# Recurrent unit of a two-layer encoder: twelve turns instead of thirteen, two products on other engines, extra turns under the other gate group

## The chip, the cores and the metric

The kernel runs on one core of a Trainium2 chip. A core has five engines with a queue each: TensorE (PE in the profile; its weight loads are listed apart as PEld), VectorE (DVE), ScalarE (ACT), GpSimd (POOL) and SyncE (SP), which here issues most DMAs. Each engine takes its own instructions in order and waits for the others by semaphores. The metric is the device time of one execution in microseconds.

## What is computed

Two layers over one sequence of 512 positions with 2048 features, in float32. The first layer (the one that the change touches) projects the normalised input into attention heads, a recurrent branch and gates, and mixes them:

```python
xc = lax.conv_general_dilated(x_lru, conv_w[:, None, :], ..., feature_group_count=LRU_WIDTH) + conv_b
y = (rg_lru(xc, wa[0], ba[0], wx[0], bx[0], lam[0], reverse=False)
     + rg_lru(xc, wa[1], ba[1], wx[1], bx[1], lam[1], reverse=True))
mix = jnp.concatenate([attn * jax.nn.silu(g_attn), y * jax.nn.silu(g_lru)], axis=-1)
return mix @ w_out
```

with, in `rg_lru` (one direction, 1024 channels in 8 blocks of 128):

```python
r = jax.nn.sigmoid(einsum(xb, wa) + ba)
i = jax.nn.sigmoid(einsum(xb, wx) + bx)
log_a = LRU_C * r * jax.nn.log_sigmoid(lam)
a = jnp.exp(log_a)
u = jnp.sqrt(-jnp.expm1(2.0 * log_a)) * (i * xc)
_, h = lax.associative_scan(lru_combine, (a, u), reverse=reverse, axis=1)   # h = a * h_before + u
```

The second layer is an mLSTM with its own projections; nothing in it is changed.

## The kernel before

**Bulk products.** All large products run in groups of 512 output columns, in steps that the code calls chunks (`NCH` = 8 per group, 256 input rows each). A weight chunk of 128 x 1024 values is loaded by SP's queue into one of three buffers (`raw`), and split into a high half `wh` (ACT, L153) and a low half `wl` (VectorE, L154), because each product is made of three passes on PE. Loads are issued three chunks ahead and splits two chunks ahead of PE (`self.ahead(i, 3, 2)`), with four buffers for the halves. A chunk of a first-layer group is 24 matmuls of 512 columns on PE, into four PSUM banks; at the last chunk the four banks are evacuated.

**Order of the groups in layer 1.** keys and values; Q0; L0 and L1 (input of the recurrence); Q1; GL0 and GL1 (gates of the recurrence, L809 and L810: a product on VectorE, a silu on ACT); GA0 and GA1 (gates of attention, same evacuation); then four groups of the output projection.

**Two lanes of small work.** While a group runs, other work is fed between its chunks from two lanes of Python generators; each `yield` ends a turn. Lane 0 (`pump(0)`) has one turn per chunk: key and query preparation, then attention (`attn_gen`: score product S, maximum L787 and L788 on VectorE, exp L791 on ACT, reciprocal L792 on VectorE, scaling L793 on ACT, transposes, split into `pth` and `ptl`, product PV). Lane 1 (`pump(1)`) has one turn at the end of each chunk: the four recurrent units `lru_gen(0)` to `lru_gen(3)`, one after the other. A group with the field `more=n` gives lane 1 a further turn, after bank 0, in each of its first n chunks. GA0 has `more=8` and GA1 none.

**A recurrent unit** handles two blocks (j) in two directions (d), each 128 x 512. Its 13 turns: two of convolution (`conv`), four of gates (`gates`: six matmuls "lg" on PE, then L880 on VectorE), one with four sigmoids (L895) and tanh (L900) on ACT and the input product i * xc on GpSimd (L903); one with exp on ACT (L908), its square on GpSimd (L911) and (square + 1) * tanh on VectorE (L912); an empty one; one with the square root on ACT (L917) and its product with the input on GpSimd (L918, 128 x 1024 each); an empty one; then the scans, a forward and a backward one per j on VectorE (L923, L925), and their sum y on GpSimd (L927), with j = 0 and j = 1 in a turn each. At the end `value_ready` multiplies y with its gate on VectorE (L832) where the gate is there already; else it stores y to DRAM (L824), to be loaded again (L818, 512 KB each way) when the gate is evacuated.

Counted by chunks, the turns of lane 1 are: 1 at L0's last chunk, 2 to 9 in L1, 10 to 17 in Q1, 18 to 25 in GL0, 26 to 33 in GL1, 34 to 49 in GA0 (two per chunk), 50 to 57 in GA1. Units 0 to 3 take turns 1 to 13, 14 to 26, 27 to 39 and 40 to 52. So unit 0's y goes through DRAM, unit 1's does not (its last turn is in GL1's first chunk).

**Splits of the mixed values.** Each chunk of the output projection needs its input split into `oh` (ACT) and `ol` (VectorE), by `mix_split`. From GA1's first chunk on, one such split stands ahead of each weight split, in the order attention 0, 1, recurrence 0, 1, 2, 3.

**Program order and issue order.** The framework orders each engine's instructions by priority (earlier in the program first) among those that its own model takes for ready. So an instruction can be issued ahead of one that stands before it in the program, and turns that lie apart can run in one block. Evacuations have a raised priority.

The activation function table of ACT is reloaded (ACT_TABLE_LOAD) where the next function isn't in the one loaded.

Of the kernel before, what the change touches and what calls it, by code (L numbers as in the profile page):

```python
# [15 lines left out]
AF = mybir.ActivationFunctionType  # L16
ALU = mybir.AluOpType
# [484 lines left out]
class Layer1(Builder):  # L502
# [344 lines left out]
    def lru_gen(self, i):  # L847
        nc, pb, v = self.nc, self.pb, self.nc.vector
        xp = self.xpad[i]
        xc = self.slot2("xc")  # L850
        hl, wh, wl = [None] * 2, [None] * 2, [None] * 2
        rr, ii = [None] * 2, [None] * 2

        def conv(j):
            b = 2 * i + j
            w = self.half("lwr")
            nc.sync.dma_start(out=w, in_=self.a["lru_w"][b])
            nc.scalar.activation(xc[:, j, :], xp[:, j, 0:512], AF.Identity,
                                 bias=pb[:, PB_CB + b:PB_CB + b + 1],
                                 scale=pb[:, PB_CW + 4 * b:PB_CW + 4 * b + 1])  # L860
            for t in range(1, 4):
                v.scalar_tensor_tensor(out=xc[:, j, :], in0=xp[:, j, t:t + 512],
                                       scalar=pb[:, PB_CW + 4 * b + t:PB_CW + 4 * b + t + 1],
                                       in1=xc[:, j, :], op0=ALU.mult, op1=ALU.add)
            hl[j] = self.slot2("xchl", F32R)
            self.split(hl[j][:, 0, :], hl[j][:, 1, :], xc[:, j, :])
            ws = self.slot2("lws", F32R)
            self.split(ws[:, 0, :], ws[:, 1, :], w)
            wh[j], wl[j] = ws[:, 0, :], ws[:, 1, :]

        def gates(j, d):
            b = 2 * i + j
            if d == 0:
                rr[j], ii[j] = self.slot2("lr"), self.slot2("li")
            for gi, (dst, off) in enumerate(((rr, PB_BA), (ii, PB_BX))):
                ps = self.psum("lg")
                ws = slice((2 * gi + d) * P, (2 * gi + d + 1) * P)
                self.mm3(ps, wh[j][:, ws], wl[j][:, ws], hl[j][:, 0, :], hl[j][:, 1, :])
                col = off + 2 * b + d
                v.tensor_scalar(out=dst[j][:, d, :], in0=ps, scalar1=pb[:, col:col + 1], scalar2=None, op0=ALU.add)  # L880

        conv(0)
        yield
        conv(1)
        yield
        gates(0, 0)
        yield
        gates(0, 1)
        yield
        gates(1, 0)  # L890
        yield
        gates(1, 1)
        yield
        for t in (rr[0], rr[1], ii[0], ii[1]):
            nc.scalar.activation(t, t, AF.Sigmoid)  # L895
        tau = [self.slot2("ltau") for j in range(2)]
        for j in range(2):
            for d in range(2):
                c = 2 * (2 * i + j) + d
                nc.scalar.activation(tau[j][:, d, :], rr[j][:, d, :], AF.Tanh, scale=self.lamc[:, c:c + 1])  # L900
        for j in range(2):
            for d in range(2):
                nc.gpsimd.tensor_tensor(out=ii[j][:, d, :], in0=ii[j][:, d, :], in1=xc[:, j, :], op=ALU.mult)  # L903
        yield
        for j in range(2):
            for d in range(2):
                c = 2 * (2 * i + j) + d
                nc.scalar.activation(rr[j][:, d, :], rr[j][:, d, :], AF.Exp, scale=self.lamn[:, c:c + 1])  # L908
            for d in range(2):
                e2 = self.half("le2")  # L910
                nc.gpsimd.tensor_tensor(out=e2, in0=rr[j][:, d, :], in1=rr[j][:, d, :], op=ALU.mult)  # L911
                v.scalar_tensor_tensor(out=tau[j][:, d, :], in0=e2, scalar=1.0, in1=tau[j][:, d, :],  # L912
                                       op0=ALU.add, op1=ALU.mult)
        yield
        yield
        for j in range(2):
            nc.scalar.activation(tau[j], tau[j], AF.Sqrt)  # L917
            nc.gpsimd.tensor_tensor(out=ii[j], in0=ii[j], in1=tau[j], op=ALU.mult)  # L918
        yield
        yield  # L920
        y = self.slot2("y")
        for j in range(2):
            v.tensor_tensor_scan(out=tau[j][:, 0, :], data0=rr[j][:, 0, :], data1=ii[j][:, 0, :],  # L923
                                 initial=0.0, op0=ALU.mult, op1=ALU.add)
            v.tensor_tensor_scan(out=tau[j][:, 1, ::-1], data0=rr[j][:, 1, ::-1], data1=ii[j][:, 1, ::-1],  # L925
                                 initial=0.0, op0=ALU.mult, op1=ALU.add)
            nc.gpsimd.tensor_tensor(out=y[:, j, :], in0=tau[j][:, 0, :], in1=tau[j][:, 1, :], op=ALU.add)  # L927
            if j == 0:
                yield
        self.mixv[4 + i] = y  # L930
        self.value_ready(4 + i)
        yield
# [57 lines left out]
class Layer2(Layer1):  # L990
# [549 lines left out]
    def build(self):  # L1540
# [14 lines left out]
        w1, wo1, w2, wo2 = a["even_w_in"], a["even_w_out"], a["odd_w_in"], a["odd_w_out"]  # L1555

        def grp(w, lo, lay, x, evac, **kw):
            return dict(w=w[:, lo:lo + 512], lay=lay, x=x, evac=evac, **kw)
# [18 lines left out]
        x1 = self.x1s.__getitem__  # L1577
# [6 lines left out]
        def after_q(g):  # L1584
            def f():
                add(0, self.q_gen(g))
                add(0, self.attn_gen(g))
            return f
# [6 lines left out]

        L = [grp(w1, 2560 + 512 * g, "T", x1, self.xlru_evac(g), after=after_lru(g)) for g in range(2)]
        Q = [grp(w1, 512 * g, "tok", x1, self.q_evac(g), after=after_q(g)) for g in range(2)]
        GA = [grp(w1, 1536 + 512 * g, "T", x1, self.gate_evac(2 * g), more=8 - 8 * g) for g in range(2)]
        GL = [grp(w1, 3584 + 512 * g, "T", x1, self.gate_evac(4 + 2 * g)) for g in range(2)]
        groups += [Q[0], L[0], L[1], Q[1], GL[0], GL[1], GA[0], GA[1]]  # L1600

# [183 lines left out]
```

## Time and profile before

| what | value | where from |
|---|---|---|
| median of 3 runs | 1645.04 us (1641.71 to 1645.58) | times |
| profiled execution | 1641.33 us, its span 1639.6 us | times, page |
| scans of unit 0 start at | 218.6, 219.8, 220.9, 222.0 us | timeline of VectorE |
| scans of unit 1 start at | 292.7, 293.9, 309.5, 310.7 us | timeline of VectorE |
| scans of unit 2 start at | 403.6, 407.5, 408.7, 409.8 us | timeline of VectorE |
| scans of unit 3 start at | 469.0, 472.3, 481.9, 483.0 us | timeline of VectorE |
| gates evacuated: GL0, GL1, GA0 (first to last) | 319.9 to 324.5, 380.8 to 385.2, 453.6 to 458.1 us | timeline of VectorE |
| PV of an attention pair on PE | 1.4 us, 12 matmuls | chain that ended last |
| four transposes on PE | 0.4 us | chain that ended last |

The profiled execution is one of four that are known; three others were only timed. All durations in the prediction come from the profiled one. Columns of a timeline: start in us, length in us, engine, line, operation, output <- inputs, shape, and in brackets the idle time of the engine before it and what ended that. A span of a GpSimd or VectorE instruction includes time in which it could not read its operands.

### The profile page before, as it was taken

The page shows a single profiled execution, that of the slowest core. Times are in us where ns is not written, and L with a number is a line of the kernel's source. Part 1 is how long each engine was busy: PE and PEld are TensorE (multiplying, and loading weights), DVE is VectorE, ACT ScalarE, POOL GpSimd, SP SyncE. Part 2 cuts the span into 40 slices and gives each one's busy share as a digit, 9 for nine tenths or more (in the row PEclk, how much of TensorE's full clock was granted, in tenths as well). Part 3 has the DMA queues.
Part 4 walks back from the last instruction along what each step waited for, and adds up shares of the span by engine and source line. Part 5 has one row for each costly group of instructions (what it writes and reads, how often), then busy time and mean ns, then how long its engine had stood idle before and what let it go on. Part 6 is the DMA issues. An engine that isn't in the chain of part 4 may idle for free.

```text
span 1639.6 us, 25389 instructions
## 1 busy us (share of the span) xinstructions
PE 1610.4 (98%) x9698; PEld 1424.1 (87%) x9698; DVE 1122.1 (68%) x1714; ACT 850.1 (52%) x1395; POOL 745.6 (45%) x732
## 2 busy tenths in 40 slices
PE   9999999999989999999999999999999999999997
PEld 7888888888768888889999999999988888888997
DVE  8755476855774333457999986666777577668976
ACT  6334665667763333334445443444576466665453
POOL 5220122303130111386698778888611322368872
PEclk9999999999989999999999999999999999999999
DMA  6433133321324544644444443444554444452565
GB/s 229 134 93 98 52 103 103 92 88 52 107 71 157 178 169 155 200 140 126 121 129 138 133 142 106 129 134 134 184 168 126 129 153 142 153 182 80 142 176 176
DMA packets 138698, 218.12 MB, mean 133 GB/s; under 512 B 9792, under 2 KB 62400, under 8 KB 138576
## 3 DMA queue, kind: packets, MB, share of 16 engines
q1 hardware_dynamic: 136304, 213.80, 41.5%
q0 software_dynamic: 1088, 2.10, 0.8%
q8 instruction: 76, 1.25, 0.3%
q10 hardware_dynamic: 1184, 0.60, 0.1%
q14 instruction: 46, 0.38, 0.1%
HBM read 182.36 MB, written 34.11 MB: 132 GB/s over the span
## 4 chain that ended last, share of the span: by engine, by line
PE 83%; DVE 6%; ACT 4%; POOL 3%; issue 3%; DMA 1%; SPq 0%; DVEq 0%; POOLq 0%; ACTq 0%
PE bk L157 44%; PE s L157 29%; DVE wl L154 2%; PE nb L157 2%; PE nf L157 1%; PE PV L157 1%; PE ST L157 1%; PE lg L157 1%; PE S L157 1%; PE tr L160 1%; ACT wh L153 1%; PE gt L157 0%; DMA hTr<-hTd 0%; DVE ltau L923 0%; DVE ltau L925 0%
## 5 line engine op out<-in xcount | busy, mean ns | idle before, releaser
L154 DVE TENSOR_TENSOR wl<-raw,wh 128x1024 fp32r<-128x1024 f32 (+3 forms) x333 | 363.4, 1093 | 267.4 <-ACT wh L153 266.7
L153 ACT CAST wh<-raw 128x1024 fp32r<-128x1024 f32 (+3 forms) x333 | 265.9, 800 | 435.7 <-PE s L157 224.5
L363 POOL TENSOR_TENSOR w7s<-raw 128x256 f32<-128x256 f32 x216 | 222.5, 1048 | 95.5 <-DMA raw<-in_odd_w_in_dram 68.2
L154 DVE TENSOR_TENSOR wl<-w7s,wh 128x512 fp32r<-128x512 f32 (+1 forms) x176 | 203.7, 1158 | 6.3 <-ACT wh L153 6.3
L157 PE MATMUL bk<-xh,wl 128*128 128x512 f32 x384 | 152.1, 396 | 5.7 <-DVE wl L154 5.7
L157 PE MATMUL s<-th,wl 128*128 128x256 f32 x544 | 153.2, 282 | 0.8 <-DVE wl L154 0.8
L157 PE MATMUL s<-th,wh 128*128 128x256 f32 x544 | 152.7, 281 | 0.5 <-ACT wh L153 0.5
L157 PE MATMUL s<-tl,wh 128*128 128x256 f32 x544 | 153.0, 281 | 0.0
L157 PE MATMUL bk<-xh,wh 128*128 128x512 f32 x384 | 152.2, 396 | 0.0
L157 PE MATMUL bk<-xl,wh 128*128 128x512 f32 x384 | 152.0, 396 | 0.0
L153 ACT CAST wh<-w7s 128x512 fp32r<-128x512 f32 (+1 forms) x176 | 125.6, 714 | 17.9 <-POOL w7s L363 17.9
L363 POOL TENSOR_TENSOR w7s<-w7s,raw 128x256 f32<-128x256 f32 x108 | 120.3, 1114 | 0.0
L157 PE MATMUL s<-bh,wh 128*128 128x256 f32 x408 | 115.3, 283 | 0.9 <-ACT wh L153 0.9
L157 PE MATMUL s<-bh,wl 128*128 128x256 f32 x408 | 114.8, 281 | 0.3 <-DVE wl L154 0.3
L157 PE MATMUL s<-bl,wh 128*128 128x256 f32 x408 | 114.4, 280 | 0.0
L903 POOL TENSOR_TENSOR li<-li,xc 128x512 f32<-128x512 f32 x16 | 21.4, 1361 | 191.9 <-ACT li L895 191.9
L363 POOL TENSOR_TENSOR w7s<-raw,w7s 128x256 f32<-128x256 f32 x108 | 101.1, 936 | 7.8
L157 PEld LDWEIGHTS s<-th,wl 128*128 128x128 f32 x544 | 102.8, 189 | 1.3 <-DVE wl L154 1.3
L157 PEld LDWEIGHTS s<-th,wh 128*128 128x128 f32 x544 | 102.4, 188 | 0.7 <-ACT wh L153 0.7
L157 PEld LDWEIGHTS s<-tl,wh 128*128 128x128 f32 x544 | 102.5, 188 | 0.0
L157 PE MATMUL bk<-oh,wh 128*128 128x512 f32 x256 | 101.0, 394 | 0.0
L157 PE MATMUL bk<-ol,wh 128*128 128x512 f32 x256 | 100.8, 394 | 0.0
(349 smaller groups left out, 4532.6 us busy)
## 6 DMA issues: line engine op xcount, KB each, us to landing
raw<-in_odd_w_in_dram SPq DMA_DIRECT2D x120, 512.0 KB, 3.9
raw<-in_even_w_in_dram SPq DMA_DIRECT2D x71, 512.0 KB, 3.7
raw<-in_even_w_out_dram SPq DMA_DIRECT2D x32, 512.0 KB, 3.7
raw<-in_odd_w_out_dram SPq DMA_DIRECT2D x32, 512.0 KB, 3.7
xres<-in_xT_dram SPq DMA_DIRECT2D x8, 512.0 KB, 6.4
x2d<-xres SPq DMA_DIRECT2D x8, 512.0 KB, 4.3
xgd<-xg SPq DMA_DIRECT2D x8, 512.0 KB, 4.0
xr<-xgd SPq DMA_DIRECT2D x8, 512.0 KB, 7.3
```

Source lines behind the costliest of these rows:

```text
L153: self.nc.scalar.copy(h, x)
L154: (eng or self.nc.vector).tensor_tensor(out=l, in0=x, in1=h.bitcast(F32), op=ALU.subtract)
L157: self.nc.tensor.matmul(out, a, b, start=start, stop=stop)
L160: self.nc.tensor.transpose(out, x, ident)
L363: po.tensor_tensor(out=s[:, :, q, :], in0=x, in1=y, op=op)
L903: nc.gpsimd.tensor_tensor(out=ii[j][:, d, :], in0=ii[j][:, d, :], in1=xc[:, j, :], op=ALU.mult)
```

## The change

It has five parts, all in layer 1.

1. The product of the root with the input (L918) is issued on VectorE instead of GpSimd.
2. The square of the exponential (L911) is issued on ACT instead of GpSimd.
3. The sum y of j = 1 is issued on VectorE instead of GpSimd; that of j = 0 stays.
4. The empty turn before the root goes, and the two turns behind it become one between root and product and one between product and scans: 12 turns per unit instead of 13.
5. GA0 no longer has additional lane-1 turns (`more=0`), and GA1 has them in its first four chunks (`more=4`).

Counted again, lane 1 has turns 34 to 41 in GA0 (one per chunk), 42 to 49 in GA1's chunks 0 to 3 (two per chunk) and 50 to 53 in its chunks 4 to 7. Units 0 to 3 take turns 1 to 12, 13 to 24, 25 to 36 and 37 to 48.

```diff
@@ -908,15 +908,15 @@
             for d in range(2):
                 e2 = self.half("le2")
-                nc.gpsimd.tensor_tensor(out=e2, in0=rr[j][:, d, :], in1=rr[j][:, d, :], op=ALU.mult)
+                nc.scalar.activation(e2, rr[j][:, d, :], AF.Square)
                 v.scalar_tensor_tensor(out=tau[j][:, d, :], in0=e2, scalar=1.0, in1=tau[j][:, d, :],
                                        op0=ALU.add, op1=ALU.mult)
         yield
-        yield
         for j in range(2):
             nc.scalar.activation(tau[j], tau[j], AF.Sqrt)
-            nc.gpsimd.tensor_tensor(out=ii[j], in0=ii[j], in1=tau[j], op=ALU.mult)
-        yield
+        yield
+        for j in range(2):
+            v.tensor_mul(ii[j], ii[j], tau[j])
         yield
         y = self.slot2("y")
         for j in range(2):
...
-            nc.gpsimd.tensor_tensor(out=y[:, j, :], in0=tau[j][:, 0, :], in1=tau[j][:, 1, :], op=ALU.add)
+            (v if j else nc.gpsimd).tensor_tensor(out=y[:, j, :], in0=tau[j][:, 0, :], in1=tau[j][:, 1, :], op=ALU.add)
             if j == 0:
                 yield
...
-        GA = [grp(w1, 1536 + 512 * g, "T", x1, self.gate_evac(2 * g), more=8 - 8 * g) for g in range(2)]
+        GA = [grp(w1, 1536 + 512 * g, "T", x1, self.gate_evac(2 * g), more=4 * g) for g in range(2)]
```

More of the change, by code (lines that the diff above doesn't have):

```diff
@@ L914, in lru_gen @@
         yield
+        for j in range(2):
+            nc.scalar.activation(tau[j], tau[j], AF.Sqrt)
         yield
         for j in range(2):
-            nc.scalar.activation(tau[j], tau[j], AF.Sqrt)
-            nc.gpsimd.tensor_tensor(out=ii[j], in0=ii[j], in1=tau[j], op=ALU.mult)
-        yield
+            v.tensor_mul(ii[j], ii[j], tau[j])
         yield
```

## The prediction

> **What bounds the kernel now.** I read the page first, then windows along the span, then what TensorE (PE) waited for, then short windows around its two holes, and last the rows of the engines that made those holes.
>
> ```profile
> span 1639.6 us, 25389 instructions
> ...
> PE 1610.4 (98%) x9698; PEld 1424.1 (87%) x9698; DVE 1122.1 (68%) x1714; ACT 850.1 (52%) x1395; POOL 745.6 (45%) x732
> ...
> 200.00:400.00 200.00, 199.60 (x960) 164.65 (x959) 133.69 (x196) 130.56 (x187) 48.75 (x36) 1.00 0.28 85
> ...
> 400.00:450.00 50.00, 46.33 (x215) 37.71 (x214) 35.84 (x51) 35.50 (x53) 12.05 (x8) 0.97 0.34 102
> 450.00:500.00 50.00, 43.30 (x192) 35.32 (x191) 34.24 (x32) 29.57 (x35) 14.26 (x9) 0.90 0.32 110
> 500.00:550.00 50.00, 50.00 (x218) 40.58 (x217) 18.05 (x17) 14.94 (x16) 0.00 (x0) 1.00 0.35 116
> ...
> PE bk L157 <- DVE wl L154: 6.4, 2, 5.7
> PE PV L157 <- DVE ptl L154: 2.9, 2, 2.7
> ```
>
> The columns of a window are its length, then busy time of PE, PEld, DVE, ACT and POOL, PE's granted clock, and the DMA. PE is 98% busy (1610.4 of 1639.6 us), so a change pays only where PE stands still or runs slowly. It idles 29.2 us in the whole span, and 3.67 + 6.70 = 10.4 us of that lie between 400 and 500 us, where the clock is also below 1. This is the stretch in which units 2 and 3 of the recurrence end. Neither neighbouring window shows such a loss. The two waits name the holes: attention's PV product waiting for its low half (ptl), and a bulk product waiting for a weight's low half (wl).
>
> ```profile
> 411.87:416.41 4.54, 0.87 (x6) 0.61 (x6) 3.21 (x6) 4.31 (x6) 1.27 (x1) 1.00 0.00 0
> 416.41:420.98 4.57, 4.57 (x18) 4.01 (x19) 4.57 (x9) 1.77 (x4) 0.00 (x0) 0.63 0.76 208
> 460.00:476.86 16.86, 10.16 (x47) 7.62 (x45) 11.18 (x9) 13.51 (x16) 8.38 (x5) 0.85 0.00 0
> 476.86:482.24 5.38, 5.38 (x19) 4.76 (x20) 5.38 (x6) 1.35 (x3) 0.00 (x0) 0.52 0.38 109
> ```
>
> Each hole costs twice: the idle time, and a slow clock behind it. Hole 1 is 4.54 - 0.87 = 3.7 us idle, then 4.57 us at clock 0.63, which loses 4.57 x 0.37 = 1.7 us: **5.4 us**. Hole 2 is 16.86 - 10.16 = 6.7 us idle, then 5.38 x 0.48 = 2.6 us: **9.3 us**. Together 14.7 us, 0.9% of the span; this is nearly all that the change can win.
>
> What made them:
>
> ```profile
> 401.16 4.77 POOL L918 TENSOR_TENSOR li<-li,ltau 128x1024 f32<-128x1024 f32 x2 [5.03 <-ACT ltau L917]
> ...
> 403.60 3.41 DVE L923 TENSOR_TENSOR_SCAN ltau<-lr,li 128x512 f32<-128x512 f32 x1 [3.03 <-POOL li L918]
> 411.93 0.13 DVE L792 RECIPROCAL att<-att 128x1 f32<-128x1 f32 x1
> 415.67 0.68 DVE L154 TENSOR_TENSOR ptl<-tr,pth 128x512 fp32r<-128x512 f32 x1
> ...
> 412.10 0.72 ACT L793 ACTIVATE pm<-pm,att 128x512 f32<-128x512 f32 x1 [6.20 <-DVE att L792]
> ```
>
> Hole 1: VectorE stands 3.03 us at the first scan until GpSimd's root product (L918) is done; that scan then takes 3.41 us while the second L918 runs, and four scans end only at 411.9. Attention's reciprocal is queued behind them, so ACT waits 6.20 us, and ptl, which PE wants, comes at 415.67.
>
> ```profile
> 443.53 1.04 ACT L153 CAST wh<-raw 128x1024 fp32r<-128x1024 f32 x1
> 464.11 1.28 ACT L917 ACT_TABLE_LOAD   x1
> 465.41 2.01 ACT L917 ACTIVATE ltau<-ltau 128x1024 f32<-128x1024 f32 x2
> 468.26 1.04 ACT L153 CAST wh<-raw 128x1024 fp32r<-128x1024 f32 x1
> ...
> 468.98 3.39 DVE L923 TENSOR_TENSOR_SCAN ltau<-lr,li 128x512 f32<-128x512 f32 x1 [3.72 <-POOL li L918]
> 474.52 2.28 DVE L154 TENSOR_TENSOR wl<-raw,wh 128x1024 fp32r<-128x1024 f32 x1
> ...
> 443.50:468.30 24.80, 24.80 (x121) 20.51 (x121) 12.69 (x19) 23.36 (x30) 8.40 (x7) 1.00 0.19 64
> ```
>
> Hole 2 has two causes in a row. ACT makes no weight half (wh) from 443.53 to 468.26: it is busy 23.36 of 24.80 us with unit 3's sigmoid, tanh, exp and root, with GA0's gates and with table loads between them. That eats the lead of two chunks. Then VectorE, 3.72 us idle before GpSimd's product and 3.39 us in a scan, makes wl only at 474.52.
>
> **The change part by part.** The groups of the recurrence, as minimum, median and maximum in ns:
>
> ```profile
> L912 DVE SCALAR_TENSOR_TENSOR ltau<-le,ltau x16: 668/686/1512, 207.3 to 464.6; 128x512 f32<-128x512 f32 x16
> L918 POOL TENSOR_TENSOR li<-li,ltau x8: 2389/2405/3407, 210.6 to 468.9; 128x1024 f32<-128x1024 f32 x8
> L923 DVE TENSOR_TENSOR_SCAN ltau<-lr,li x8: 1192/1214/3409, 218.6 to 481.9; 128x512 f32<-128x512 f32 x8
> L911 POOL TENSOR_TENSOR le<-lr x16: 1039/1041/1354, 202.0 to 463.5; 128x512 f32<-128x512 f32 x16
> L927 POOL TENSOR_TENSOR y<-ltau x8: 1272/1532/2188, 223.4 to 484.3; 128x512 f32<-128x512 f32 x8
> L832 DVE TENSOR_TENSOR mixr<-mixr,gate x5: 1214/1215/1225, 322.7 to 516.5; 128x1024 f32<-128x1024 f32 x5
> ```
>
> *Root's product to VectorE.* GpSimd loses 8 x 2.4 us. VectorE gains 8 products of the shape and operation of L832, 1.2 us each. On the chain from root to scan that is 1.2 instead of 2.4 us per half, and the scan beside it should take 1.2, not 3.4 us: 1.2 + 2.2 = 3.4 us shorter in each of units 2 and 3. What queues behind the product, should it wait for the root, is attention's small work and wl; a turn now lies between root and product, so I take that wait at nothing. Uncovered it is at most the 3 to 4 us that the scan waits now.
>
> The Trainium skill (SBUF — State Buffer, Who interferes with whom) says that a VectorE instruction with two SBUF inputs and a GpSimd one that reads SBUF shut each other out for a whole instruction. The 3.41 us scan beside L918 agrees; by that rule the moved product can be caught too, by GpSimd's remaining input product, for some 2.5 us in a unit, and the gain would be that much less where it happens on the path.
>
> *Squares to ACT.*
>
> ```profile
> 294.77 1.28 ACT L908 ACT_TABLE_LOAD   x1
> 298.72 0.63 ACT L671 ACTIVATE sqt<-qraw 128x512 f32<-128x512 f32 x1
> ```
>
> The square of L671 has the same shape: 0.63 us, and it runs after the exponential's load without a load of its own. So 4 x 0.63 = 2.5 us more on ACT per unit, no further loads, and 4 x 1.04 us off GpSimd. L912 no longer waits for another engine's queue, and its slowest, 1.51 us, should fall to 0.69. In units 0 and 1, whose last scans start at 222.0 and 310.7 us (table above), all this is hidden: PE is busy 199.60 of 200 us between 200 and 400.
>
> The Trainium skill (ScalarE: Activation LUTs, What ACT_TABLE_LOAD costs) adds a drain of 1.38 us to each load of 1.28. The rows differ: the root's load at 464.11 is followed by the root at 465.41 with 0.02 us between. By the page, four loads in GA1 would add 5.5 us of ACT time to the residue below; I go by the rows.
>
> *y's second sum on VectorE:* 0.7 us (half of L832's elements) instead of GpSimd's 1.3 to 2.2 us and a crossing between engines; the product with the gate follows on the same engine.
>
> *Turns.* A unit takes 12 turns instead of 13, and lane 1 gets one turn per chunk in GA0, two in GA1's first four. By counting, unit 2 then has its root at GL1's end and product and scans in GA0's chunks 0 to 2, one turn each (before: exp to scans, turns 34 to 39, in the same three chunks at two each). Unit 3's convolutions and gates fill GA0's chunks 3 to 7 and GA1's first turn; sigmoid to scans come in GA1's chunks 0 to 3, behind the evacuation of GA0 and no longer across it. What I expect: VectorE has about 2.4 us of scans or products per chunk, not 8.4 us in a block, so hole 1 goes (5.4 us). For hole 2, the exponentials of attention and the silu of GA0's gates leave the stretch of unit 3, with two to four table loads of 1.28 us.
>
> What is late next is GA1's chunk 4. ACT then holds, by the rows below, sigmoid 5.3 (a load and four of 1.0), tanh 2.6 (four of 0.66), exp 3.9 (a load and four like tanh), squares 2.5 and root 3.3 us (a load and 2.01): 17.6 in all. About 7 us of weight halves, mix halves (oh, each like a wh of 1.04) and attention's rest come on top: 24.6 us.
>
> ```profile
> 303.14 5.56 PE bk L157 x24
> ...
> 435.59 1.06 ACT L895 ACTIVATE lr<-lr 128x1024 f32<-128x1024 f32 x1
> 448.42 1.32 ACT L900 ACTIVATE ltau<-lr,lamc 128x512 f32<-128x512 f32 x2
> ...
> 443.55 0.73 DVE L880 TENSOR_SCALAR li<-lg,pb 128x512 f32<-128x512 f32 x1
> ```
>
> Three chunks of 5.6 us and attention's rest on PE (1.4 + 0.4, table above) last 18.6 us, so in strict order chunk 4 would miss its halves by some 6 to 7 us. But the order on an engine is not strict: half a unit's sigmoid now runs at 435.6, eight microseconds before VectorE hands over the other half's last gate (443.55), though it stands behind it in the program. Between 0 and 7 us (9 with a slow clock behind it) I take **3 us** left.
>
> *Unit 1* now ends in GL0's chunk 6 (was GL1's chunk 0), before its gate exists, so its y makes a trip through DRAM that it didn't make: one store and one load, like unit 0's.
>
> ```profile
> 229.10 0.46 SPq L824 DMA_DIRECT2D mixd<-y  x1
> 317.60 0.42 SPq L818 DMA_DIRECT2D mixr<-mixd  x1
> DMA to landing us min/median/max: 5.1/5.1/5.1
> DMA to landing us min/median/max: 4.9/5.6/6.0
> ```
>
> 5.1 + 5.6 = 10.7 us and two issues in SP's queue, where weight loads follow. Weights lie a chunk ahead of their split and the split two ahead of PE (17 us), so I take 0; at worst VectorE's product with the gate waits 5 us in GL1's first chunk, still inside that lead.
>
> **Sum:** -5.4 - 9.3 + 3 = -11.7 us. The profiled execution took 1641.3 us (span 1639.6), so 1629.6. The three timed runs and this one average 1643.4, with a median of 1645.0; adding the 2 us by which the average lies above the profiled one gives **1632**.
>
> **Rivals.**
> 1. *Only one hole closes.* The framework reorders: unit 0's and unit 2's four scans ran in one block (table above) though a turn lies between them. If hole 2 stays, the gain is 5.4 us: 1641.3 - 5.4 + 2 = 1638. For it: ACT's 23.36 busy of 24.80 us, to which squares are added. Against it: fewer loads, and the gates' silu is out of the way.
> 2. *The hole moves.* ACT's 24.6 us in GA1 take the place of the block before, and a hole of 7 us with its slow clock, plus late wl behind the scans (4 x 1.2 us), gives back 14 us: 1643, no change.
> 3. *Slower.* Place: GA1's chunks 3 to 5. If ACT takes all of unit 3 from sigmoid to root ahead of chunk 3's wh, it is ready 17.6 + 2.1 (two mix halves) + 1.9 (attention's rest) + 3 (the root waiting for VectorE, as the scan does now) + 2.2 (wh, wl) = 26.8 us after chunk 0, while PE wants it after two chunks and a PV, 12.6 us: 14 us idle and 2.6 at the slow clock. Chunks 4 and 5 then find no lead and wait for 2 x 2.1 us of halves: 21 us against 14.7 won, 1641.3 + 6.3 + 2 = 1650. It decides from 15 us of delay on; now the same kind of gap cost 9.3.
>
> **Chances.** Forecast (gain 6 to 15 us) 0.56, rival 1 0.15, rival 2 0.17, rival 3 0.12. The range reaches from both holes gone with nothing left (1641.3 - 14.7 = 1626.6) to rival 2 at the upper runs, 1645; rival 3 and a few per cent below stay out. A measurement here tells about 0.3% (4.9 us) from no change; rival 1 falls on either side of that. Faster 0.66, same 0.21, slower 0.13.
>
> **What would show it.** Right: PE's wait for ptl near 412 gone; scans at 1.2 us without a 3.4 us one; PE idle between 400 and 500 us at 4 us or less; squares at 0.6 us without a load before them; clock 1 over GA0. Wrong: a wait of PE for wl of over 5 us in GA1's chunks 3 to 5 with ACT over 95% busy ahead of it; VectorE idle at the product waiting for ACT's root; a wait at GL1's start for unit 1's reload; or scans again in one block in GA0.

## The result, and the profile after

The changed kernel takes 1631.98 us (median of 4 runs, 1629.1 to 1633.51) against 1645.31 us before (4 runs, 1641.71 to 1649.2). The ratio is 0.9916, with a 95% interval of 0.989 to 0.9943: 0.8% faster. The profiled execution took 1629.1 us, 12.2 us less than the 1641.33 us of the one before. Among the runs of the experiments below, one of only_more (6616.68 us) and one of only_squares (4094.48 us) lie far outside the others and are left out of medians and ratios.

The page of the changed kernel, then its windows (same columns as before):

```profile
span 1627.2 us, 25384 instructions
...
PE 1608.7 (99%) x9698; PEld 1424.1 (88%) x9698; DVE 1118.2 (69%) x1726; ACT 856.7 (53%) x1410; POOL 703.0 (43%) x704
```

```profile
200.00:400.00 200.00, 198.67 (x951) 163.54 (x949) 134.25 (x205) 140.19 (x203) 20.78 (x18) 1.00 0.28 87
...
400.00:450.00 50.00, 49.96 (x251) 41.82 (x252) 34.53 (x55) 32.58 (x51) 4.63 (x3) 1.00 0.44 137
450.00:500.00 50.00, 50.00 (x227) 40.96 (x226) 37.32 (x39) 35.53 (x43) 5.70 (x3) 1.00 0.36 119
```

PE is busy for all but 0.04 of the 100 us in which it idled 10.4 us before, and the granted clock is 1.00 instead of 0.97 and 0.90. Both holes are gone, with the slow clock behind them. One small new hole lies in the window ahead (198.67 instead of 199.60 us busy). PE's waits from 380 to 500 us (total, times, longest):

```profile
PE S L157 <- ACT attn L774: 1.1, 1, 1.1
PE PV L157 <- DVE ptl L154: 0.3, 1, 0.3
```

How much this is worth can be read at one place: the start of the last bulk matmul on the layer's input, the end of GA1. It stands as the last start in the row of that group in the view by tile, here for the kernel before and then for the changed one:

```profile
L157 PE MATMUL bk<-xh,wl x384: 387/393/797, 101.3 to 512.9; 128*128 128x512 f32 x192
```

```profile
L157 PE MATMUL bk<-xh,wl x384: 387/393/401, 101.7 to 498.8; 128*128 128x512 f32 x192
```

The gates' last product starts 14.1 us earlier, and no matmul of the group takes 797 ns any more (393 is its median; the longest is 401). I call this time **the gates' end** below. Two profiled executions of the changed kernel agree on it within 0.1 us, two of only_more (below) within 0.6 us, whereas their whole spans differ by 2 to 3 us, which the last section explains in part. So it is the sharper measure of what happens in layer 1, and the timed ratios say whether it arrives at the end.

VectorE at the second root product of unit 2 and in unit 3, and ACT around unit 3. The root's product stands in line 919 of the changed kernel, the root in 916, the square in 911:

```profile
395.78 1.23 DVE L919 TENSOR_TENSOR li<-li,ltau 128x1024 f32<-128x1024 f32 x1 [2.09 <-ACT ltau L916]
...
470.38 2.36 DVE L919 TENSOR_TENSOR li<-li,ltau 128x1024 f32<-128x1024 f32 x2 [1.93 <-ACT ltau L916]
472.66 1.22 DVE L154 TENSOR_TENSOR ol<-mixr,oh 128x1024 fp32r<-128x1024 f32 x1
473.79 1.22 DVE L154 TENSOR_TENSOR wl<-raw,wh 128x1024 fp32r<-128x1024 f32 x1
474.93 1.22 DVE L923 TENSOR_TENSOR_SCAN ltau<-lr,li 128x512 f32<-128x512 f32 x1
```

```profile
445.18 1.04 ACT L895 ACTIVATE li<-li 128x1024 f32<-128x1024 f32 x1
...
450.48 1.06 ACT L153 CAST wh<-raw 128x1024 fp32r<-128x1024 f32 x1
...
464.24 1.14 ACT L911 ACTIVATE le<-lr 128x512 f32<-128x512 f32 x2
...
472.07 2.94 ACT L153 CAST wh<-raw 128x1024 fp32r<-128x1024 f32 x3
```

The product takes 1.2 us per half (two in 2.36), the scan behind it 1.22 instead of 3.39 us, and the weight's low half (wl) stands between product and scans, not behind them. VectorE now waits about 2 us ahead of the product for ACT's root, in unit 2 as in unit 3. And ACT still makes no weight half (wh) from 450.48 to 472.07 us: a gap of 21.6 us instead of 24.7 us. That the holes vanish while these two stay is what the experiments had to explain.

### The profile page after: what moved, and what is told of

It reads as the page before. It is cut to its first block, busy times and chain, and to the rows that moved or that the text cites. A ratio compares the mean times of both kernels' runs of the same rounds, so it can differ in the third digit from the quotient of the medians.

```text
span 1627.2 us, 25384 instructions
## 1 busy us (share of the span) xinstructions
PE 1608.7 (99%) x9698; PEld 1424.1 (88%) x9698; DVE 1118.2 (69%) x1726; ACT 856.7 (53%) x1410; POOL 703.0 (43%) x704
## 4 chain that ended last, share of the span: by engine, by line
PE 84%; DVE 4%; ACT 4%; issue 3%; POOL 3%; DMA 2%; SPq 0%; DVEq 0%; POOLq 0%; ACTq 0%
PE bk L157 45%; PE s L157 30%; DVE wl L154 2%; PE nb L157 1%; PE lg L157 1%; PE nf L157 1%; PE PV L157 1%; PE S L157 1%; PE ST L157 1%; PE tr L160 1%; DMA x2d<-x 1%; ACT wh L153 1%; PE gt L157 0%; POOL hfb L1328 0%; POOL ts L549 0%
## 5 line engine op out<-in xcount | busy, mean ns | idle before, releaser
L363 POOL TENSOR_TENSOR w7s<-w7s,raw 128x256 f32<-128x256 f32 x108 | 116.1, 1075 | 0.0
```

Of the source, the lines that this page charges most:

```text
L363: po.tensor_tensor(out=s[:, :, q, :], in0=x, in1=y, op=op)
```

## The experiments

Question one: which part closes the holes, the turns, the engines, or only both together? Question two: which of the causes that the prediction named makes each hole? All kernels are variants of the kernel before unless said otherwise. The table gives all twelve runs; ratios and medians are against runs of the kernel before on the same chip.

| run | what differs from before | us (before) | ratio, 95% | gates' end, us against 512.9 | PE idle and clock, 400 to 500 us |
|---|---|---|---|---|---|
| only_engines | product, second y, squares moved; turns as before | 1633.32 (1645.81) | 0.9928, 0.9913 to 0.9943 | -8.4 | 4.89, 0.98 |
| only_turns | 12 turns and GA1's extra turns; engines as before | 1634.67 (1645.81) | 0.9936, 0.9921 to 0.9951 | -10.9 | 1.52, 1.00 |
| more_undone | the change, extra turns under GA0 as before | 1636.34 (1645.81) | 0.9946, 0.9929 to 0.9962 | -8.6 | 3.69, 0.98 |
| only_more | only the extra turns moved to GA1 | 1628.95 (1645.81) | 0.9896, 0.9879 to 0.9913 | -14.4 | 0.64, 1.00 |
| gate2_later | unit 2's product with its gate put off | 1644.41 (1643.8) | 1.0001, 0.9991 to 1.001 | -0.2 | 10.38, 0.93 |
| unit3_waits | four empty turns in unit 3 | 1634.8 (1643.8) | 0.9947, 0.9931 to 0.9963 | -9.5 | 3.68, 0.98 |
| only_product | only the root's product on VectorE | 1630.39 (1643.8) | 0.9921, 0.9907 to 0.9936 | -13.0 | 1.92, 1.00 |
| only_squares | only the squares on ACT | 1644.73 (1643.8) | 1.0004, 0.9995 to 1.0014 | +1.8 | 10.11, 0.93 |
| gate2_out | unit 2's product with its gate left out | 1644.09 (1645.6) | 0.9989, 0.9979 to 0.9998 | -1.8 | 8.82, 0.97 |
| after_again | the change | 1632.47 (1645.6) | 0.9927, 0.9915 to 0.9938 | -14.1 | 0.02, 1.00 |
| only_more_again | as only_more | 1630.31 (1645.6) | 0.9914, 0.9901 to 0.9926 | -15.0 | 0.63, 1.00 |
| more_product | only_more, with product and second y moved | 1630.44 (1645.6) | 0.9908, 0.9893 to 0.9922 | -16.4 | 0.00, 1.00 |

The idle time of the last column is 100 us less PE's busy time in a window's row. In most runs the gates' end agrees with the ratio: -14.1 us is 0.86% of 1645, and the change measures 0.84 and 0.73%; -9.5 us is 0.58%, and unit3_waits measures 0.53%. only_engines is the exception: -8.4 us is 0.51%, and its ratio gives 0.72% (0.57 to 0.87%).

### The halves of the change

**only_engines**

```diff
-                nc.gpsimd.tensor_tensor(out=e2, in0=rr[j][:, d, :], in1=rr[j][:, d, :], op=ALU.mult)
+                nc.scalar.activation(e2, rr[j][:, d, :], AF.Square)
...
-            nc.gpsimd.tensor_tensor(out=ii[j], in0=ii[j], in1=tau[j], op=ALU.mult)
+            v.tensor_mul(ii[j], ii[j], tau[j])
...
-            nc.gpsimd.tensor_tensor(out=y[:, j, :], in0=tau[j][:, 0, :], in1=tau[j][:, 1, :], op=ALU.add)
+            (v if j else nc.gpsimd).tensor_tensor(out=y[:, j, :], in0=tau[j][:, 0, :], in1=tau[j][:, 1, :], op=ALU.add)
```

> The three moves between engines alone (root's product and the second sum y on VectorE, squares on ACT), with the 13 turns and the 8 additional turns in GA0 of before. Theory A (both parts matter: the moves shorten the chain from root to scan by 3.4 us a unit, the turns take unit 3's ACT work away from GA0's evacuation): hole 1 near 412 us shrinks from 5.4 us to 0 to 2, hole 2 near 470 us from 9.3 to 3 to 6 because ACT's long stretch without a weight half stays; 6 to 9 us faster than before. Theory B (the moves alone do it): no hole left, 12 to 14 us faster. Theory C (the turns alone do it): holes as before, 0 to 3 us faster.

**only_turns**

```diff
         yield
-        yield
         for j in range(2):
             nc.scalar.activation(tau[j], tau[j], AF.Sqrt)
-            nc.gpsimd.tensor_tensor(out=ii[j], in0=ii[j], in1=tau[j], op=ALU.mult)
         yield
+        for j in range(2):
+            nc.gpsimd.tensor_tensor(out=ii[j], in0=ii[j], in1=tau[j], op=ALU.mult)
         yield
...
-        GA = [grp(..., self.gate_evac(2 * g), more=8 - 8 * g) for g in range(2)]
+        GA = [grp(..., self.gate_evac(2 * g), more=4 * g) for g in range(2)]
```

> The turns alone (12 per unit, none additional in GA0, four in GA1), with product, squares and y on GpSimd as before. Theory A: hole 1 goes nearly, because the scans stand a chunk apart, and of hole 2 some 2 to 5 us stay because VectorE still waits 3 to 4 us for GpSimd's product: 8 to 12 us faster than before. Theory B: 0 to 3 us faster. Theory C: 12 to 14 us faster.

**more_undone**, from the changed kernel:

```diff
-        GA = [grp(..., self.gate_evac(2 * g), more=4 * g) for g in range(2)]
+        GA = [grp(..., self.gate_evac(2 * g), more=8 - 8 * g) for g in range(2)]
```

> The change with GA0's eight additional turns back (and GA1 without). With 12 turns per unit, all of unit 3 then ends in GA0, one turn ahead of its end. Theory A: sigmoid, exp and root of unit 3 meet attention's exponentials in GA0's last three chunks, so ACT makes 2 to 4 more table loads there; a hole of 2 to 6 us comes back, 6 to 11 us faster than before. Theory B (the moves alone do it): same as the changed kernel, 12 to 14 us faster. Theory C: holes come back whole, 0 to 4 us faster.

**only_more**, from the kernel before:

```diff
-        GA = [grp(..., self.gate_evac(2 * g), more=8 - 8 * g) for g in range(2)]
+        GA = [grp(..., self.gate_evac(2 * g), more=4 * g) for g in range(2)]
```

> The additional turns alone moved from GA0 to GA1's first four chunks; 13 turns per unit and all work on its engine of before. Unit 3 then takes turns 40 to 52 and ends in GA1's chunk 6. Theory A: hole 1 shrinks to 0 to 3 us (one turn per chunk in GA0), hole 2 to 2 to 6 us, later in GA1: 6 to 12 us faster than before. Theory B: 0 to 3 us faster. Theory C: as much as the turns alone, 10 to 14 us faster; unit 3's mix split must still be in time for the output projection's sixth chunk.

*Measured.* Each half alone gives most of the gain: 8.4 and 10.9 us at the gates' end, 19.3 together, where the whole change gives 14.1. And the one line of only_more gives 14.4 us by itself. The parts are no sum; they are several ways to the same two holes. By their ratios, only_turns (10.5 us) and more_undone (8.9 us) fall into Theory A's range. only_engines (11.8 us) lies above it, though its gates' end lies within. only_more (17 us) gained more than any of the theories gave it.

only_more is also a test of the prediction's reading of hole 1, since it leaves unit 2's block of scans together and GpSimd's product ahead of it (the block ends 0.8 us earlier than before). VectorE there, in units 2 and 3:

```profile
404.44 3.41 DVE L923 TENSOR_TENSOR_SCAN ltau<-lr,li 128x512 f32<-128x512 f32 x1 [0.92 <-POOL li L918]
...
410.00 1.19 DVE L925 TENSOR_TENSOR_SCAN ltau<-lr,li 128x512 f32<-128x512 f32 x1
411.12 0.13 DVE L792 RECIPROCAL att<-att 128x1 f32<-128x1 f32 x1
411.17 1.20 DVE L154 TENSOR_TENSOR wl<-raw,wh 128x1024 fp32r<-128x1024 f32 x1
412.51 0.69 DVE L154 TENSOR_TENSOR ptl<-tr,pth 128x512 fp32r<-128x512 f32 x1
...
418.38 1.22 DVE L832 TENSOR_TENSOR y<-y,gate 128x1024 f32<-128x1024 f32 x1
...
479.44 3.39 DVE L923 TENSOR_TENSOR_SCAN ltau<-lr,li 128x512 f32<-128x512 f32 x1 [2.31 <-POOL li L918]
```

and PE's waits there, from 380 to 500 us:

```profile
PE PV L157 <- DVE ptl L154: 0.3, 1, 0.3
PE tr L160 <- ACT pm L793: 0.3, 1, 0.3
```

The block of four scans is there, 3.41 us scan and all, the reciprocal is queued behind it, and PE waits 0.64 us instead of 3.67. What is missing between reciprocal and ptl is unit 2's product with its gate (L832), which here came at 418.38 us. Also in unit 3 the scan of 3.39 us and the wait for GpSimd stay, and PE doesn't notice. So neither of the two that the prediction set out to remove from VectorE, the long scan and the wait for GpSimd, costs PE more than those 0.64 us by itself.

only_turns and only_engines each show one remaining weakness. In only_turns ACT has a gap of 22.7 us (wh at 451.84, then at 474.57 us) and GpSimd still the product: PE waits 1.52 us for wl. In only_engines, with unit 3 still across GA0's end, the gap is 34.5 us:

```profile
426.51 1.05 ACT L153 CAST wh<-raw 128x1024 fp32r<-128x1024 f32 x1 [1.78 <-PE bk L157]
...
460.99 1.03 ACT L153 CAST wh<-raw 128x1024 fp32r<-128x1024 f32 x1
...
426.50:461.00 34.50, 32.49 (x161) 26.75 (x159) 17.10 (x29) 33.38 (x44) 5.10 (x4) 1.00 0.18 59
```

ACT is busy 33.38 of 34.50 us, and PE waits 3.1 us for wh. So a long enough gap of ACT makes a hole alone, with no scan in the way; one of 22 us needs something more.

In more_undone unit 3's scans come, with two turns per chunk, directly ahead of GA0's evacuation on VectorE, and PE waits 3.57 us for the evacuation (L809), not for ACT as Theory A had it. So under GA0 the extra turns cost the shorter unit a wait, and under GA1 they cost it none; the 13-turn unit gains from the move as well (only_more).

### What makes each hole

**gate2_later** and **gate2_out**: two edits of unit 2's product with its gate, on which only_more had thrown suspicion.

```diff
         self.mixd[i] = d
+        if i == 6:
+            self.later.append(partial(self.try_mix, i))
+            return
         self.try_mix(i)
```

> Before, with one thing moved: unit 2's product of y with its gate (1.2 us on VectorE, which waits 1.3 us for GpSimd's y ahead of it) is put off to the start of GA1. The scans, GpSimd's products and all turns stay. Theory D (formed from the run with only the additional turns moved, where the scans stood in the same block and one took 3.41 us as before, yet no hole was left near 412 us): not the block of scans but this product and the weight half behind it kept attention's ptl back. Hole 1 shrinks from 5.4 us to 0.5 to 2, hole 2 stays at 8 to 11; 3 to 5 us faster than before. The prediction's reading (block of scans): hole 1 stays above 4 us; 0 to 1 us faster.

```diff
-            self.nc.vector.tensor_mul(self.mixv[i], self.mixv[i], self.gate.pop(i))
+            gate = self.gate.pop(i)
+            if i != 6:
+                self.nc.vector.tensor_mul(self.mixv[i], self.mixv[i], gate)
```

> Before, with unit 2's product of y and its gate left out (that quarter of the recurrent branch goes on ungated). The run that only put it off in the program is no test, since the instruction was issued at the same place. Theory D (this product, and VectorE's wait for GpSimd's y ahead of it, keep ptl back): PE's wait for ptl near 416 us falls from 2.68 us to 0.3 or less, the 0.99 us wait ahead of it (for the scaling, behind the scans) stays, no slow clock follows; hole 2 stays at 9 us; 4 to 5 us faster than before. The prediction's reading (the block of scans alone): the wait for ptl stays above 2 us; 0 to 1 us faster.

*Measured.* gate2_later was no test. The product stands later in the program, but was issued at the same place (413.11 us, after a wait of 1.33 us for GpSimd's y), since the framework places it by its own model. Both holes are as before (10.38 us idle). gate2_out leaves unit 2's y without its gate. VectorE, then PE, then a window:

```profile
413.16 0.13 DVE L792 RECIPROCAL att<-att 128x1 f32<-128x1 f32 x1
413.21 1.20 DVE L154 TENSOR_TENSOR wl<-raw,wh 128x1024 fp32r<-128x1024 f32 x1
414.55 0.69 DVE L154 TENSOR_TENSOR ptl<-tr,pth 128x512 fp32r<-128x512 f32 x1
```

```profile
414.10 0.66 PE L160 MATMUL tr<-ident,pm 128*128 128x128 f32 x4 [1.03 <-ACT pm L793]
...
415.30 0.39 PE L157 MATMUL PV<-ptl,vh 128*128 128x256 f32 x1 [0.34 <-DVE ptl L154]
```

```profile
410.00:425.00 15.00, 12.85 (x59) 9.55 (x58) 14.86 (x21) 9.46 (x15) 4.29 (x2) 1.00 0.38 112
```

In the kernel before, VectorE's rows between reciprocal and ptl are these; the first is the suspect:

```profile
413.39 1.22 DVE L832 TENSOR_TENSOR y<-y,gate 128x1024 f32<-128x1024 f32 x1 [1.33 <-POOL y L927]
414.54 1.22 DVE L154 TENSOR_TENSOR wl<-raw,wh 128x1024 fp32r<-128x1024 f32 x1
```

Without it PE's wait for ptl falls from 2.68 to 0.34 us, and the clock behind it stays 1.00 (0.63 before). The 1.0 us wait ahead of it (the transposes wait for pm, whose reciprocal is queued behind the scans) stays. So 2.3 of hole 1's 3.67 us need this product (1.22 us, and 1.33 us of waiting for GpSimd's sum y). They need not be due to it alone: GpSimd forms that sum behind the last scan of the block (412.09 us), and only_product, below, closes the hole with the product and its wait still there. The gain at the gates' end is only 1.8 us, against the 4 to 5 us expected: the order around it shifted too, and PE waits 1.8, 0.5 and 0.2 us in new places (ptl, then the small products of unit 3).

**unit3_waits**: hole 2 by ACT's gap, or by GpSimd's product and the long scan, which would take the hole along?

```diff
         yield
+        for _ in range(4 if i == 3 else 0):
+            yield
         for t in (rr[0], rr[1], ii[0], ii[1]):
```

> Before, with four empty turns in unit 3 alone ahead of its sigmoid, so that sigmoid to scans fall into GA1's chunks 0 to 6 instead of across GA0's evacuation; the additional turns stay in GA0 and all work on its engine. Theory A (ACT's stretch at the boundary makes hole 2): hole 2 shrinks from 9.3 us to 0 to 2 and fewer table loads stand between 434 and 468 us than the nine of before; hole 1 stays at 5 us; 7 to 9 us faster. Rival (GpSimd's product and VectorE's wait for it make hole 2): the hole moves along with the scans into GA1 and keeps 5 us or more; 0 to 4 us faster.

*Measured.* In this kernel the lines below the edit are numbered two higher. Its ACT and its VectorE:

```profile
450.09 1.05 ACT L153 CAST wh<-raw 128x1024 fp32r<-128x1024 f32 x1 [0.23 <-PE bk L157]
...
455.71 1.04 ACT L153 CAST wh<-raw 128x1024 fp32r<-128x1024 f32 x1
...
469.08 1.05 ACT L153 CAST wh<-raw 128x1024 fp32r<-128x1024 f32 x1
```

```profile
475.15 3.43 DVE L154 TENSOR_TENSOR wl<-raw,wh 128x1024 fp32r<-128x1024 f32 x1
478.51 3.42 DVE L925 TENSOR_TENSOR_SCAN ltau<-lr,li 128x512 f32<-128x512 f32 x1
```

The longest gap is now 13.4 us instead of 24.7. Beside GpSimd's product VectorE's wl takes 3.43 us and its scan 3.42 us, one behind the other, worse than before. Hole 2 is gone all the same: 3.68 us idle between 400 and 500 us is hole 1 alone. The hole did not go along with the product.

**only_product** is the counterpart: the gap stays, and VectorE's wait and long scan go.

```diff
-            nc.gpsimd.tensor_tensor(out=ii[j], in0=ii[j], in1=tau[j], op=ALU.mult)
+            v.tensor_mul(ii[j], ii[j], tau[j])
```

> Before, with the root's product alone on VectorE (squares and both sums y stay on GpSimd, turns as before). The prediction gives it 3.4 us on the chain of units 2 and 3: hole 1 from 5.4 to 0 to 2 us, hole 2 from 9.3 to 4 to 6; 7 to 9 us faster. Rival (it is the squares, or the order that the framework makes of them, that helped the run with all moves between engines): 0 to 3 us faster.

*Measured.* Its ACT and its VectorE:

```profile
438.81 1.04 ACT L153 CAST wh<-raw 128x1024 fp32r<-128x1024 f32 x1
...
463.52 1.04 ACT L153 CAST wh<-raw 128x1024 fp32r<-128x1024 f32 x1
```

```profile
461.76 2.36 DVE L918 TENSOR_TENSOR li<-li,ltau 128x1024 f32<-128x1024 f32 x2 [1.24 <-ACT ltau L917]
464.04 1.22 DVE L154 TENSOR_TENSOR ol<-mixr,oh 128x1024 fp32r<-128x1024 f32 x1
465.18 1.22 DVE L154 TENSOR_TENSOR wl<-raw,wh 128x1024 fp32r<-128x1024 f32 x1
```

ACT's gap is 24.7 us, the same as before, and the wl behind it starts 1.66 us after its wh (465.18 - 463.52). In the kernel before it took 6.26 us (474.52 - 468.26): VectorE stood 3.72 us idle and 3.39 us in the scan. PE's wait for wl, 5.71 us before, is gone; of its 6.70 us of idle time only the 0.95 us for attention's pth are left (0.99 before). **Hole 2 is made by two things in conjunction**: a gap of ACT of about 25 us uses up the lead of two chunks, and VectorE then adds 4.6 us that nothing covers any more. Take away either and it closes. The gain of 13 us is more than the 7 to 9 expected, since that expectation kept 4 to 6 us of hole 2.

Hole 1 closes here too. Product and scans are spread (L918 at 400.57, scans from 404.71 to 409.43 us), and attention's reciprocal and its ptl come between them:

```profile
408.07 0.13 DVE L792 RECIPROCAL att<-att 128x1 f32<-128x1 f32 x1
...
408.71 0.68 DVE L154 TENSOR_TENSOR ptl<-tr,pth 128x512 fp32r<-128x512 f32 x1
...
412.95 1.22 DVE L832 TENSOR_TENSOR y<-y,gate 128x1024 f32<-128x1024 f32 x1 [1.12 <-POOL y L927]
```

The product with the gate still waits 1.12 us for GpSimd's y, and PE doesn't notice, because the ptl stands ahead of it. So hole 1 is made by two things as well: the block of scans holds attention's small work back, and the product with the gate then keeps ptl waiting. The block without the product behind it left 0.64 us (only_more) and 1.37 us (gate2_out), the product without the block left no wait for ptl (only_product).

**only_squares**: does this part do anything by itself?

```diff
-                nc.gpsimd.tensor_tensor(out=e2, in0=rr[j][:, d, :], in1=rr[j][:, d, :], op=ALU.mult)
+                nc.scalar.activation(e2, rr[j][:, d, :], AF.Square)
```

> Before, with the squares alone on ACT (2.5 us more ACT per unit, turns as before). Theory A: ACT is 23.36 of 24.80 us busy ahead of hole 2, so that hole grows by 0 to 3 us and hole 1 stays: 0 to 3 us slower than before. Rival (the squares' wait for GpSimd was on the path): 2 to 5 us faster.

*Measured.* No gain (ratio 1.0004, 0.9995 to 1.0014), and the gates' end is 1.8 us later. Hole 2, which was expected to grow, keeps a wait of 5.19 us for wl (5.71 before). PE's new waits lie in unit 0, and hole 1 is larger:

```profile
219.10 0.51 PE L157 MATMUL S<-kTh,qT 128*128 128x512 f32 x1 [1.47 <-DVE ptl L154]
226.78 0.66 PE L160 MATMUL tr<-ident,pm 128*128 128x128 f32 x4 [1.14 <-ACT pm L793]
...
416.27 0.66 PE L160 MATMUL tr<-ident,pm 128*128 128x128 f32 x4 [2.25 <-ACT pm L793]
419.81 0.58 PE L157 MATMUL PV<-ptl,vh 128*128 128x256 f32 x1 [2.68 <-DVE ptl L154]
```

### Which version is best

**more_product** joins the two single edits that paid most, with the second y; squares and number of turns as before. It was run on one chip with the changed kernel and with only_more, both again and unedited (after_again, only_more_again).

```diff
-            nc.gpsimd.tensor_tensor(out=ii[j], in0=ii[j], in1=tau[j], op=ALU.mult)
+            v.tensor_mul(ii[j], ii[j], tau[j])
...
-            nc.gpsimd.tensor_tensor(out=y[:, j, :], in0=tau[j][:, 0, :], in1=tau[j][:, 1, :], op=ALU.add)
+            (v if j else nc.gpsimd).tensor_tensor(out=y[:, j, :], in0=tau[j][:, 0, :], in1=tau[j][:, 1, :], op=ALU.add)
...
-        GA = [grp(..., self.gate_evac(2 * g), more=8 - 8 * g) for g in range(2)]
+        GA = [grp(..., self.gate_evac(2 * g), more=4 * g) for g in range(2)]
```

> Before with the additional turns moved, and the root's product and y's second sum on VectorE; squares stay on GpSimd, 13 turns. If the parts added up (14.4 us to the end of layer 1 by the turns, 13.0 by the product): 25 us or more faster than before. As each closes the same two holes of 14.7 us: 13 to 17 us faster, no PE wait above 0.5 us between 200 and 560 us, and within 0.15% of the run with only the turns moved.

> The changed kernel once more, beside the two below on the same chip. 12 to 15 us faster than before (0.991 to 0.993).

> Before with the additional turns alone moved from GA0 to GA1, once more. If this single edit is all that the holes need, and the other four parts of the change add nothing: 13 to 17 us faster than before, equal to the changed kernel within 0.2% or up to 3 us ahead of it (no 1.1 us hole at GA0's start, no squares on ACT). If the first measurement was luck: 10 to 12 us faster, behind the changed kernel.

*Measured.* more_product has no wait of PE over 0.2 us between 200 and 560 us, and its gates' end is the earliest (-16.4 us). In time the three are close: 0.9908, 0.9914 and 0.9927, with intervals that overlap. The medians of the two simpler versions are 2 us lower than the change's (1632.47 us), and their gates' end is earlier; that they are faster is not settled.

The change's own new hole (1.07 us at 391.25 us, PE's score product waiting for ACT's copy L774) goes with the unit of 12 turns. It is in all three kernels that have it (1.07, 1.08 and 1.60 us, the last with 1.58 us more at 391.4) and in no run of 13 turns. The shorter unit puts unit 2's root among GL1's gates, and ACT then loads tables at 383.19, 385.64, 388.49 and 391.21 us, 1.28 us each.

## Why the prediction was right, and where its reasons were not

**The sum** was -11.7 us for the profiled execution; it measured -12.2. There is luck in how near that is. The gates' end moved by 14.1 us, 2.4 more than the sum, and the rest of that execution gave 1.9 us back. The change's second profiled execution (after_again), with the same gates' end, took 1632.14 us, which is 9.2 us less than the one before. The 2 us between profiled and average run came out near too (1629.1 against an average of 1631.6), but other kernels show no such rule: only_turns' profiled run lies 0.5 us above its median, more_product's 0.9 us.

**Holes 1 and 2, 5.4 and 9.3 us:** the sizes, slow clock included, were right. 14.7 us were to be won there, and the gates' end moved by 14.1, with 1.4 us of new waiting in the small holes at 391 and 400 us. Reading idle time and granted clock from windows was the step that carried the forecast.

**Hole 1 had a second cause, which the prediction left out.** It took the step "VectorE has about 2.4 us of scans or products per chunk, not 8.4 us in a block, so hole 1 goes". It went, and breaking up the block is enough to close it, as only_product shows. But the block is not enough to make it. only_more keeps the block and its 3.41 us scan, and the hole shrinks to 0.64 us; gate2_out keeps the block too and takes away 2.3 of 2.68 us of PE's longer wait. The row that was missing is L832, on VectorE between the reciprocal and ptl, with its wait for GpSimd's y. The prediction quoted the rows on either side of it and left it out, so it read two delays as one. The 1.0 us of the hole ahead of it, attention's pm, may be the block's; that part was not tried alone.

**Hole 2's causes were named rightly, their logic was not.** The prediction had both rows, ACT's 24.8 us without wh and VectorE's wait and 3.39 us scan, and counted on the change to relieve both. unit3_waits and only_product show that relieving one is enough. So rival 1 (one hole stays) had less behind it than it was given: the product alone and the extra turns alone each close both holes but for 1 or 2 us of idle time.

**The residue of 3 us in GA1's chunk 4 did not come.** Its counting gave ACT 24.6 us against 18.6 us of PE's work. ACT's gap measured 21.6 us. Of these the recurrence took 16.9 us, not 17.6: half the sigmoids ran ahead of the gap (445.18 us above), but the exponentials came in two groups with a load of the table each. That leaves about 4.7 us for weight halves, mix halves and attention's rest, where the prediction took 7. On PE the last two groups of unit 3's small products, about 1.4 us each, fell into the gap: 18.6 + 2.8 = 21.4 us. By the same counting nothing is left. That is read from this one trace and wasn't tried by itself. So one half of the miss was work that PE turned out to have there, and most of the other half was the 7 us, taken too high.

**The product's wait for the root, taken at nothing,** was 2.09 us in unit 2 and 1.93 us in unit 3 (the brackets of L919). The prediction had named this as a sign of being wrong. It cost little: behind it PE waited 0.29 us for ptl in unit 2, and nothing in unit 3.

**Product, scans, squares, y** ran near the forecast prices: 1.2 us, 1.2 us, 0.62 us (two, overlapping, in 1.14, without a load of their own) and 0.68 us. No product took more than 1.23 us, so none was caught beside GpSimd's input product. "All this is hidden" in units 0 and 1 held within the change. Alone, the squares cost 1.8 us at the gates' end, in unit 0 among other places, and no run shows a gain from them.

**Unit 1's trip through DRAM at 0** held: those two small holes are PE's only waits over 0.2 us between 200 and 560 us. Rivals 2 and 3 (ACT's work in GA1 as a new hole) did not occur; only_turns came nearest, with 1.52 us.

## What to carry to other kernels

When a wait ends on a chain through two engines, count how much of the lead each uses up: two delays that make a hole together can be worth the whole hole each, so try the cheapest edit alone before the large one. Ahead of the operand that PE waited for, read every row of the engine that made it, not only the longest. Parts of a change that aim at the same hole do not add, and one that aims at none (here the squares) brought no gain that any run shows.

## What the runs showed of the hardware

*The clock behind a hole.* Behind 2.68 us of idle (with 0.99 shortly before) the granted clock was 0.63 over 4.57 us, behind 5.71 us 0.52 over 5.38 us; behind 3.57 us, in more_undone, 0.65 over 4.9 us; behind 3.08 us, in only_engines, 0.73 over 6.4 us. The stretch behind 5.71 us lost 2.6 us, the other three 1.7 us each. Behind single holes of 1.78 us (gate2_out) and 1.52 us (only_turns) the clock stayed 1.00. But the length of one hole doesn't decide: in layer 2 (below) four short waits, 1.55 us in all, had a slow stretch behind them that also lost 1.7 us. So these rows give the price of a slow stretch and no sharp threshold. The Trainium skill (TensorE: Matmul & The Clock Gate, Part 1: The HAM clock gate) gives a window of about 3.4 us of idle, and the same of work to return. At half clock (0.50 from 418 to 420 us in the kernel before) a loss of 1.7 us takes 3.4 us, which agrees with the return; the idle time does not agree, as 3.08 us in one piece and 1.55 us in four were enough.

*Unchanged work varies by more than the differences looked for.* In layer 2 the engines' instructions stand in the same order in the kernel before, the change, only_more, only_engines and only_turns. Yet two executions of the changed kernel, whose layer 2 begins within 0.1 us of the same time, end their last group of this kind 2.6 us apart:

```profile
L157 PE MATMUL s<-th,wh x544: 274/281/386, 729.6 to 1587.2; 128*128 128x256 f32 x182
```

```profile
L157 PE MATMUL s<-th,wh x544: 274/281/415, 729.5 to 1589.8; 128*128 128x256 f32 x182
```

Most of that lies in one place. The same 12 us in the first and in the second execution:

```profile
1490.00:1502.00 12.00, 11.21 (x92) 10.80 (x91) 10.59 (x16) 9.92 (x19) 6.96 (x8) 1.00 0.50 176
```

```profile
1490.00:1502.00 12.00, 10.45 (x71) 9.61 (x70) 10.59 (x17) 9.63 (x18) 6.90 (x9) 0.86 0.49 172
```

The second idles 0.76 us more there, in four waits for wh and wl within 3.2 us instead of two, and loses 12 x 0.14 = 1.68 us to a slow clock behind them: 2.4 of the 2.6 us. Why there were more waits is open. Across those five kernels the group takes from 856.9 us (only_engines) to 860.8 us (only_turns) from its first start to its last. Spans of single executions can't rank kernels that differ by less.

*A shared wait is not a cost.* A scan of 1.2 us took 3.4 us, and a wl of 1.2 us also 3.4 us, beside GpSimd's 2.4 us product. The Trainium skill (SBUF — State Buffer, Who interferes with whom) says that a VectorE instruction with two SBUF inputs contends with a GpSimd one that reads SBUF; these rows agree. But in unit 3 of only_more and of unit3_waits PE never noticed.
